# Strassen groups of the SwiGLU downs: weight sums as additions, two of four made by adding DMAs

## The chip, the core and the metric

The kernel runs on one NeuronCore of a Trainium2 chip. TensorE multiplies matrices, VectorE and ScalarE work element by element, GpSimd is used for small things, SyncE issues transfers, and 16 DMA engines move data between DRAM and the on-chip memory. The metric is the device time of one execution in microseconds (us), less is better.

## The reference

One decoder layer for 256 tokens of width 1024, in float32: a SwiGLU feed-forward, a mixer of two parallel branches (a state-space branch and differential attention), and a second feed-forward, each between two RMS norms. The part that matters here is the feed-forward, which occurs twice:

```python
def swiglu(x, w_gate, w_up, w_down):          # x: 256 x 1024, d_ff = 2816
    return (jax.nn.silu(x @ w_gate) * (x @ w_up)) @ w_down

h = h + 0.5 * rmsnorm(swiglu(rmsnorm(h, ffn1_pre_g[l]), ffn1_w_gate[l], ffn1_w_up[l], ffn1_w_down[l]), ffn1_post_g[l])
```

The product with `w_down` (2816 x 1024) is called the downs.

## The kernel before

**Precision.** Each float32 operand is split into a high part (a rounding copy on ScalarE, `whi` or `wqh`) and a low part (the difference, on VectorE, `wlo` or `wql`). A product is three TensorE products: high by high, high by low, low by high.

**Weights.** All weights arrive as chunks of 1 MB, in a list made ahead of time (`chunks`). SyncE issues their loads in that order (`load_to`, L238) into three buffers, `raw`. A chunk's buffer is given to the chunk three places on as soon as the chunk is split, so a load waits on the split that empties its buffer, and everything behind it on SyncE's queue waits too. The split parts go into a pool of 29 buffers of 4 KB per partition (`k4`), which TensorE empties by using them. Splits run ahead of their use by three chunks (`AHEAD`).

**The downs.** The rows of `w_down` make eleven chunks of 256 rows. Six of them form three Strassen groups of two chunks (class `Quad`); the order of work is the string `DOWN`: group, plain chunk, group, plain chunk, group, three plain chunks. A group is a 2 x 2 block product: two halves of its 512 rows by two halves of the 1024 columns. Quarters 0 and 1 are the left and right half of its first chunk, 2 and 3 those of its second. Seven products of 128 x 512 outputs replace eight, so a group takes 42 matmuls where its two chunks alone would take 48; a product needs either a quarter or a sum of quarters as weights. Products 1, 2 and 3 take quarters 0, 2 and 3. Products 5, 6, 7 and 4 take sums, which VectorE makes by subtraction (L122): 5 is quarter 1 less quarter 0, 6 is quarter 3 less sum 5, 7 is quarter 3 less quarter 1, and 4 is quarter 2 less sum 6. Each is one instruction on 128 x 1024 elements into a k4 buffer named `wt`. The products run in the order `FIRST` in the first two groups of a feed-forward and `LAST` in the third:

```python
FIRST, LAST = (1, 2, 3, 5, 7, 6, 4), (1, 6, 7, 2, 5, 3, 4)
```

The activations have sums of their own (`sums_of`, L674 to L677), and at the end `combine` adds product banks (L721).

**What sets the order.** Where the kernel calls `own_order`, the named engines run in the order in which the program records its instructions; elsewhere a planner of the framework orders them by costs of its own. Each engine takes its instructions strictly in order. The splits of the first group stand between the last gate and up products, whose banks (`pj`, three of them) ScalarE and VectorE empty (L330, L331).

**The end of the downs.** The last three plain chunks are held (`TAIL`), and their products run first for the upper 128 tokens, then for the lower, so that the upper block's norm runs beside the lower block's products. The gain row for the norm is loaded by GpSimd's queue (L587).

Of the kernel before, what the change touches and what calls it, by code (L numbers as in the profile page):

```python
# [19 lines left out]
ALU = mybir.AluOpType  # L20
# [6 lines left out]
P = 128  # L27
T = 256
# [26 lines left out]
def tile_hybrid_layer(ctx: ExitStack, tc: tile.TileContext, x, ffn1_pre_g, ffn1_w_gate, ffn1_w_up,  # L55
# [4 lines left out]
    nc = tc.nc  # L60
# [5 lines left out]
    def k4(shape, name, dt=F32):  # L66
        return sb.tile(shape, dt, tag="k4", name=name, bufs=K4_BUFS)
# [25 lines left out]
    class Quad:  # L93

        PLAIN = {1: 0, 2: 2, 3: 3}
        SUMS = {5: (1, 0), 6: (3, 5), 7: (3, 1), 4: (2, 6)}

        def __init__(self, i, products):  # L100
            self.i, self.sums, self.products = i, {}, products
            self.uses = [[p for p in products if p in (1, 5)], [p for p in products if p in (5, 7)],
                         [p for p in products if p in (2, 4)], [p for p in products if p in (3, 6, 7)]]

        def quarter(self, n, p):

            self.uses[n].remove(p)
            return raws[self.i + n // 2][:, :, (n % 2) * 512:(n % 2 + 1) * 512]

        def give_back(self):  # L110
            for j in range(2):
                if raws[self.i + j] is not None and not self.uses[2 * j] and not self.uses[2 * j + 1]:
                    raws[self.i + j] = None
                    load_to(self.i + j + 1 + RAW_BUFS)

        def sum_of(self, p):

            if p not in self.sums:
                n, m = self.SUMS[p]
                m = self.sum_of(m) if p in (6, 4) else self.quarter(m, p)  # L120
                t = k4([P, 2, 512], f"wt{self.i}{p}")
                nc.vector.tensor_sub(t, self.quarter(n, p), m)  # L122
                self.sums[p] = t
            return self.sums[p]

        def split(self, p):
            load_to(self.i + 2)
            hi = k4([P, 2, 512], f"wqh{self.i}{p}", F32R)
            src = self.quarter(self.PLAIN[p], p) if p in self.PLAIN else self.sum_of(p)
            nc.scalar.copy(hi, src)  # L130
            for later in self.products[self.products.index(p) + 1:][:1]:
                if later in self.SUMS:
                    self.sum_of(later)
            lo = k4([P, 2, 512], f"wql{self.i}{p}", F32R)
            nc.vector.tensor_sub(lo, src, hi.bitcast(F32))  # L135
            self.give_back()
            return lambda kt: hi[:, kt, :], lambda kt: lo[:, kt, :]

    chunks, units = [], []

    def chunk(src, shape):
        units.append((len(chunks), None))
# [8 lines left out]
    def n_chunk(w, k0):  # L153
        chunk(w[k0:k0 + 2 * P, :].rearrange("(j p) c -> p j c", p=P), [P, 2, D])

    def quad(w, k0, products):

        n = len(units)
        for k in (k0, k0 + 2 * P):
            n_chunk(w, k)  # L160
        del units[n:]
        q = Quad(len(chunks) - 2, products)
        units.extend((q, p) for p in products)


# [53 lines left out]
    raws, splits = [], []  # L219
# [11 lines left out]
    def load_to(n):  # L231
        while len(raws) < min(n, len(chunks)):
            i = len(raws)
            src, shape = chunks[i]
            r = sb.tile(shape, F32, tag="raw", name=f"raw{i}", bufs=RAW_BUFS)
            nj = shape[1] // 4 if i == 0 else shape[1] // 2 if i < 4 else shape[1]
            for j in range(0, shape[1], nj):
                nc.sync.dma_start(r[:, j:j + nj, :], src[:, j:j + nj, :])  # L238
            raws.append(r)

    def split_steps(ahead=True):


        i, _ = units[len(splits)]
        load_to(i + 1)
        r, shape = raws[i], chunks[i][1]
        nj = shape[1] // 2
        his, los = [], []
        splits.append((his, los))
        for q in range(2):  # L250
            hi = k4([P, nj, shape[2]], f"whi{i}{q}", F32R)
            lo = k4([P, nj, shape[2]], f"wlo{i}{q}", F32R)
            his.append(hi)
            los.append(lo)
            n = 1 if i == 0 else nj
            for j in range(0, nj, n):
                js = slice(j, j + n)
                copy = nc.scalar.copy if i + q + j else nc.vector.tensor_copy
                behind(copy(hi[:, js, :], r[:, q * nj + j:q * nj + j + n, :]), "cast")  # L259
                if not i + q + j:  # L260
                    yield
                m = nc.vector.tensor_sub(lo[:, js, :], r[:, q * nj + j:q * nj + j + n, :], hi[:, js, :].bitcast(F32))  # L262
# [404 lines left out]
    def sums_of(g, even, odd):  # L667


        bs = (slice(0, P), slice(P, T))  # L670
        v = k4([P, 4, 2, P], f"sv{g}")
        hi, lo = ((k3 if g < 3 else k4)([P, 3, 2, P], f"s{n}{g}", F32R) for n in "hl")
        more = k2([P, 2, 2, P], f"s4{g}", F32R)
        nc.vector.tensor_tensor(v[:, 0], even[:, :, bs[1]], odd[:, :, bs[1]], ALU.add)  # L674
        nc.vector.tensor_sub(v[:, 2], even[:, :, bs[0]], even[:, :, bs[1]])
        nc.vector.tensor_sub(v[:, 1], v[:, 0], even[:, :, bs[0]])
        nc.vector.tensor_sub(v[:, 3], odd[:, :, bs[0]], v[:, 1])  # L677
        split(hi, lo, v[:, 0:3])
        split(more[:, 0], more[:, 1], v[:, 3])
        return ([hi[:, i] for i in range(3)] + [more[:, 0]], [lo[:, i] for i in range(3)] + [more[:, 1]])  # L680

    def mm_quads(acts, sums, tag):


        bank = {p: bg([P, 512], f"acc_{tag}p{p}") for p in (2, 3, 5, 4, 8)}
        bank.update({p: pj(f"acc_{tag}p{p}") for p in (1, 6, 7)})
        acc = [[bank[2], bank[3]], [bank[4], bank[8]]]
        begun, n_quads = set(), max(n for n, (kind, j) in enumerate(down[tag]) if kind == "q") + 1
        of_quads = down[tag][:n_quads]

        def mm(p, x_, w_, last):
            nc.tensor.matmul(bank[p], x_, w_, start=p not in begun, stop=last and p in (1, 5, 6, 7))  # L692
            begun.add(p)

        for n, (kind, j) in enumerate(of_quads):
            last = n == n_quads - 1
            if kind == "p":
                wh, wl = take()
                for kt in range(2):
                    ah, al = acts[2 * j + kt]  # L700
                    for b in range(2):
                        ts = slice(b * P, (b + 1) * P)
                        for x_, w_ in ((ah, wh), (al, wh), (ah, wl)):
                            for q in range(2):
                                p = ((2, 3), (4, 8))[b][q]
                                mm(p, x_[:, ts], w_(kt)[:, halves[q]], False)
                continue
            sh, sl = sums[j]
            for p in LAST if last else FIRST:
                wh, wl = take()  # L710
                for kt in range(2):
                    if p in (1, 2, 4):
                        k, b = {1: (0, 0), 2: (2, 0), 4: (2, 1)}[p]
                        ah, al = (x_[:, b * P:(b + 1) * P] for x_ in acts[4 * j + k + kt])
                    else:
                        ah, al = (x_[{5: 0, 6: 1, 7: 2, 3: 3}[p]][:, kt, :] for x_ in (sh, sl))
# [287 lines left out]
    for o, n, off in ((0, P, 0), (P, T, P)):  # L1004
        v = dneg[:, o:o + n]
# [371 lines left out]
    class Background:  # L1377
# [5 lines left out]
        def add(self, g):  # L1383
            self.q.append(g)
# [183 lines left out]
```

## Time and profile before

| what | value |
|---|---|
| median of three runs | 734.62 us (733.73 to 734.84) |
| profiled execution, span from first to last instruction | 732.0 us |
| TensorE busy | 724.0 us (99%) |
| VectorE busy | 609.2 us (83%) |
| ScalarE busy | 475.3 us (65%) |
| moved by DMA | 137.92 MB, mean 188 GB/s |

The profile gives the execution's span; what lies around it is the 2.6 us by which the median is longer. A row of a timeline has the start and the duration in us, the engine, the line of the kernel, the operation, and output <- inputs with shapes; a bracket at its end tells how long the engine had been idle and what ended that. PE is TensorE, DVE VectorE, ACT ScalarE, POOL GpSimd, SP SyncE. The first feed-forward's downs run from 130 to 190 us, those of the second from 666 to 725 us; their first chunks are loaded from 110 and from 646 us on.

### The profile page before, as it was taken

How to read it: one execution, taken by the hardware profiler on the slowest of the kernel's cores; microseconds unless marked ns; L12 is line 12 of the kernel's file. 1: busy time of each engine (PE TensorE's matmuls, PEld its weight loads, DVE VectorE, ACT ScalarE, POOL GpSimd, SP SyncE). 2: the span in 40 equal slices, each digit the busy share in tenths (PEclk: the TensorE clock that was granted, in tenths of full speed). 3: DMA queues.
4: the chain of work that ended last, by engine and by line, in shares of the span. 5: the costliest groups of instructions: out<-in, count | busy, mean ns of one | idle time of the engine just before them, and what ended most of it. 6: DMA issues, size and time to landing. Idle time of an engine off the chain costs nothing.

```text
span 732.0 us, 10570 instructions
## 1 busy us (share of the span) xinstructions
PE 724.0 (99%) x4025; PEld 618.4 (84%) x4025; DVE 609.2 (83%) x948; ACT 475.3 (65%) x815; POOL 37.0 (5%) x66
## 2 busy tenths in 40 slices
PE   9999999999999999999999999999999999999996
PEld 7888888888878889999888888888888888888885
DVE  6978787999979999877996997784784878779995
ACT  6656566656867676869965577772663657566562
POOL 2800000000200000000000000000010000000000
PEclk9999999999999999999999999999999999999999
DMA  8874645467673647666564664475471664654541
GB/s 290 241 247 157 225 146 203 173 210 279 182 228 118 201 146 250 187 192 207 159 221 146 215 209 147 140 246 187 129 238 35 231 195 153 227 205 145 185 185 57
DMA packets 94210, 137.92 MB, mean 188 GB/s; under 512 B 2684, under 2 KB 68304, under 8 KB 94160
## 3 DMA queue, kind: packets, MB, share of 16 engines
q1 hardware_dynamic: 91488, 129.51, 53.1%
q0 software_dynamic: 2368, 7.22, 3.2%
q8 instruction: 31, 0.51, 0.3%
q10 hardware_dynamic: 304, 0.53, 0.2%
q14 instruction: 19, 0.16, 0.1%
HBM read 136.17 MB, written 1.08 MB: 188 GB/s over the span
## 4 chain that ended last, share of the span: by engine, by line
PE 99%; DVE 0%; ACT 0%; DVEq 0%; issue 0%; ACTq 0%
PE pup_f L326 9%; PE pg_f L326 9%; PE pws L345 6%; PE pgt L345 6%; PE acc_f1p L692 5%; PE acc_f2p L692 5%; PE pxs L326 4%; PE pg_f L325 4%; PE pup_f L325 4%; PE pn_f L355 3%; PE acc_mx L614 3%; PE pn_mx L345 3%; PE pn_f L345 3%; PE pwd L345 3%; PE acc_f1p L614 2%; PE acc_f2p L614 2%
## 5 line engine op out<-in xcount | busy, mean ns | idle before, releaser
L262 DVE TENSOR_TENSOR wlo<-raw,whi 128x1024 fp32r<-128x1024 f32 (+1 forms) x222 | 262.2, 1209 | 19.5 <-ACT whi L259 18.3
L259 ACT CAST whi<-raw 128x1024 fp32r<-128x1024 f32 (+1 forms) x221 | 222.8, 1043 | 12.8 <-PE psc L1255 2.5
L326 PE MATMUL pup_f<-u_f,whi 128*128 128x512 f32 x288 | 101.5, 396 | 0.0
L326 PE MATMUL pg_f<-u_f,whi 128*128 128x512 f32 x288 | 101.3, 396 | 0.0
L325 PE MATMUL pg_f<-u_f,wlo 128*128 128x256 f32 x252 | 70.6, 280 | 0.0
L325 PE MATMUL pup_f<-u_f,wlo 128*128 128x256 f32 x252 | 70.3, 279 | 0.0
L326 PEld LDWEIGHTS pup_f<-u_f,whi 128*128 128x128 f32 x288 | 52.9, 188 | 9.9
L326 PEld LDWEIGHTS pg_f<-u_f,whi 128*128 128x128 f32 x288 | 52.8, 188 | 9.7
L325 PEld LDWEIGHTS pg_f<-u_f,wlo 128*128 128x128 f32 x252 | 47.5, 189 | 1.7
L325 PEld LDWEIGHTS pup_f<-u_f,wlo 128*128 128x128 f32 x252 | 47.5, 189 | 1.6
L326 PE MATMUL pxs<-u_mx,whi 128*128 128x512 f32 x128 | 44.6, 397 | 0.0
L130 ACT CAST wqh<-wt 128x1024 fp32r<-128x1024 f32 x24 | 25.3, 1054 | 23.3 <-DVE wt L122 22.1
L330 ACT COPY su_f<-pup_f 128x256 f32<-128x256 f32 x36 | 13.4, 372 | 37.5 <-PE pup_f L326 37.4
L331 DVE TENSOR_TENSOR su_f<-pup_f,su_f 128x256 f32<-128x256 f32 x36 | 15.1, 421 | 25.0 <-ACT su_f L330 24.9
L345 PE MATMUL pgt<-whi,u_mx 128*128 128x512 f32 x128 | 33.1, 393 | 0.0
L311 PE MATMUL pz<-u_mx,whi 128*128 128x256 f32 x128 | 31.8, 285 | 0.0
L312 PE MATMUL pz<-u_mx,whi 128*128 128x256 f32 x128 | 31.4, 283 | 0.0
L325 PE MATMUL pxs<-u_mx,wlo 128*128 128x256 f32 x112 | 31.2, 279 | 0.0
L135 DVE TENSOR_TENSOR wql<-wt,wqh 128x1024 fp32r<-128x1024 f32 x24 | 29.2, 1218 | 0.2
L345 PEld LDWEIGHTS pgt<-whi,u_mx 128*128 128x128 f32 x128 | 23.6, 188 | 5.3 <-issue 0.7
L326 PEld LDWEIGHTS pxs<-u_mx,whi 128*128 128x128 f32 x128 | 23.2, 188 | 4.2
L301 ACT CAST gh_f<-sg_f 128x512 fp32r<-128x512 f32 x18 | 11.2, 620 | 23.0 <-DVE sg_f L848 23.0
(415 smaller groups left out, 1699.1 us busy)
## 6 DMA issues: line engine op xcount, KB each, us to landing
raw<-in_w_in_dram SPq DMA_DIRECT2D x40, 1024.0 KB, 5.2
raw<-in_ffn_w_down_dram SPq DMA_DIRECT2D x22, 1024.0 KB, 4.9
raw<-in_ffn_w_gate_dram SPq DMA_DIRECT2D x20, 1024.0 KB, 5.2
raw<-in_ffn_w_up_dram SPq DMA_DIRECT2D x20, 1024.0 KB, 5.2
raw<-in_ssd_w_branch_dram SPq DMA_DIRECT2D x8, 1024.0 KB, 4.9
acb<-acd POOLq DMA_DIRECT2D x8, 512.0 KB, 5.0
raw<-in_da_w_branch_dram SPq DMA_DIRECT2D x4, 1024.0 KB, 4.9
raw<-in_w_out_dram SPq DMA_DIRECT2D x4, 1024.0 KB, 4.9
```

Of the source, the lines that this page charges most:

```text
L130: nc.scalar.copy(hi, src)
L135: nc.vector.tensor_sub(lo, src, hi.bitcast(F32))
L259: behind(copy(hi[:, js, :], r[:, q * nj + j:q * nj + j + n, :]), "cast")
L262: m = nc.vector.tensor_sub(lo[:, js, :], r[:, q * nj + j:q * nj + j + n, :], hi[:, js, :].bitcast(F32))
L311: nc.tensor.matmul(acc[m], wh(j)[:, cs], ah(k0 + j), start=first and j == ks[0], stop=False)
L312: nc.tensor.matmul(acc[m], wh(j)[:, cs], al(k0 + j), start=False, stop=False)
L325: nc.tensor.matmul(acc[:, :T], wl(j)[:, cs], ah(j), start=False, stop=False)
L326: nc.tensor.matmul(acc, wh(j)[:, cs], ahl(j), start=j == 0, stop=j == KD - 1)
L345: nc.tensor.matmul(acc, a(k0 + j), b(j), start=first and i == 0, stop=last and i == 11)
L355: nc.tensor.matmul(accs[b], x_(k0 + j), w_(j), start=first and j == 0 and w_ is wh and x_ is acts[b][0], stop=last and j == 3 and w_ is wl)
L614: nc.tensor.matmul(acc[b][q][:, cs] if to is None else to, x_[:, ts], w_(kt)[:, halves[q]][:, cs], start=to is not None and kt == 0 and x_ ...
L692: nc.tensor.matmul(bank[p], x_, w_, start=p not in begun, stop=last and p in (1, 5, 6, 7))
```

## The change

The signs of the group's intermediate products are turned so that every sum of weights is an addition. Product 5 now takes quarter 0 + quarter 1, product 7 takes quarter 1 + quarter 3, product 6 takes quarter 0 + sum 7, product 4 quarter 2 + sum 6. The first two are made while loading: right after the group's first chunk has been issued, GpSimd issues a DMA that adds quarter 0 from DRAM onto quarter 1 in the chunk's buffer; SyncE loads quarter 1 once more into a k4 buffer, and GpSimd issues a DMA that adds quarter 3 from DRAM onto it. Quarter 1 is thus only used by product 5, and quarter 3 only by product 3 and, from DRAM, by sum 7. A sum's k4 buffer is taken when the chunk is loaded, not when VectorE would have made the sum. Sums 6 and 4 stay on VectorE. In the activations' sums and in `combine`, additions and subtractions change places.

```diff
-        PLAIN = {1: 0, 2: 2, 3: 3}
-        SUMS = {5: (1, 0), 6: (3, 5), 7: (3, 1), 4: (2, 6)}
+        PLAIN = {1: 0, 5: 1, 2: 2, 3: 3}
...
-            self.uses = [[p for p in products if p in (1, 5)], [p for p in products if p in (5, 7)],
-                         [p for p in products if p in (2, 4)], [p for p in products if p in (3, 6, 7)]]
+            self.uses = [[p for p in products if p in (1, 6)], [5], [p for p in products if p in (2, 4)], [3]]
...
+        def of_dram(self, k, c):
+            return self.w[self.k0 + k * T:self.k0 + (k + 1) * T, c * 512:(c + 1) * 512].rearrange(
+                "(j p) c -> p j c", p=P)
+
+        def added(self):
+
+            nc.gpsimd.dma_start(raws[self.i][:, :, 512:], self.of_dram(0, 0), accum_op=ALU.add)
+            t = self.sums[7] = k4([P, 2, 512], f"wt{self.i}7")
+            nc.sync.dma_start(t, self.of_dram(0, 1))
+            nc.gpsimd.dma_start(t, self.of_dram(1, 1), accum_op=ALU.add)
...
-                n, m = self.SUMS[p]
-                m = self.sum_of(m) if p in (6, 4) else self.quarter(m, p)
+                n, m = {6: (0, 7), 4: (2, 6)}[p]
+                m = self.sum_of(m)
                 t = k4([P, 2, 512], f"wt{self.i}{p}")
-                nc.vector.tensor_sub(t, self.quarter(n, p), m)
+                nc.vector.tensor_tensor(t, self.quarter(n, p), m, ALU.add)
...
             raws.append(r)
+            if i in quads:
+                quads[i].added()
...
-        nc.vector.tensor_tensor(v[:, 0], even[:, :, bs[1]], odd[:, :, bs[1]], ALU.add)
+        nc.vector.tensor_sub(v[:, 0], even[:, :, bs[1]], odd[:, :, bs[1]])
...
-        nc.vector.tensor_sub(v[:, 3], odd[:, :, bs[0]], v[:, 1])
+        nc.vector.tensor_tensor(v[:, 3], odd[:, :, bs[0]], v[:, 1], ALU.add)
...
-            add(u4, bank[5], u2)
-            add(c4, bank[5], u3)
+            nc.vector.tensor_sub(u4, bank[5], u2)
+            nc.vector.tensor_sub(c4, bank[5], u3)
```

In each engine's list of instructions, VectorE has 850 rows before and 838 after, GpSimd 70 and 82, SyncE 127 and 133; TensorE has the same 3220, of which in each feed-forward two (the first two matmuls of the first group's product 2) move from between the last two up-products' halves to behind them.

More of the change, by code (lines that the diff above doesn't have):

```diff
@@ L93, in tile_hybrid_layer, with __init__ @@
     class Quad:
-        PLAIN = {1: 0, 2: 2, 3: 3}
-        SUMS = {5: (1, 0), 6: (3, 5), 7: (3, 1), 4: (2, 6)}
-        def __init__(self, i, products):
-            self.i, self.sums, self.products = i, {}, products
-            self.uses = [[p for p in products if p in (1, 5)], [p for p in products if p in (5, 7)],
-                         [p for p in products if p in (2, 4)], [p for p in products if p in (3, 6, 7)]]
+        PLAIN = {1: 0, 5: 1, 2: 2, 3: 3}
+        def __init__(self, i, w, k0, products):
+            self.i, self.w, self.k0, self.sums, self.products = i, w, k0, {}, products
+            self.uses = [[p for p in products if p in (1, 6)], [5], [p for p in products if p in (2, 4)], [3]]
         def quarter(self, n, p):
@@ L131, in split @@
             for later in self.products[self.products.index(p) + 1:][:1]:
-                if later in self.SUMS:
+                if later in (4, 6):
                     self.sum_of(later)
@@ L137, in split @@
             return lambda kt: hi[:, kt, :], lambda kt: lo[:, kt, :]
-    chunks, units = [], []
+    chunks, units, quads = [], [], {}
     def chunk(src, shape):
@@ L161, in quad @@
         del units[n:]
-        q = Quad(len(chunks) - 2, products)
+        q = quads[len(chunks) - 2] = Quad(len(chunks) - 2, w, k0, products)
         units.extend((q, p) for p in products)
```

## The prediction

> **What bounds the kernel now.** I read the page first (busy shares, then the chain that ended last), then TensorE's waits, then the stretch of the first feed-forward's downs in windows.
>
> ```profile
> span 732.0 us, 10570 instructions
> PE 724.0 (99%) x4025; PEld 618.4 (84%) x4025; DVE 609.2 (83%) x948; ACT 475.3 (65%) x815; POOL 37.0 (5%) x66
> ...
> PE 99%; DVE 0%; ACT 0%; DVEq 0%; issue 0%; ACTq 0%
> ```
> ```profile
> PE warm L425 <- DVE zeros L408: 1.1, 1, 1.1
> PE pn_f L355 <- DVE raw_u L478: 0.3, 1, 0.3
> ```
> ```profile
> core 0: us, PE busy (x) PEld busy (x) DVE busy (x) ACT busy (x) POOL busy (x), PEclk, DMA share, GB/s
> 110.00:120.00 10.00, 10.00 (x59) 8.73 (x58) 7.79 (x10) 7.28 (x11) 0.00 (x0) 1.00 0.65 221
> 120.00:130.00 10.00, 10.00 (x60) 8.69 (x58) 8.13 (x11) 5.64 (x8) 0.00 (x0) 1.00 0.38 147
> 130.00:140.00 10.00, 10.00 (x50) 8.40 (x49) 9.93 (x12) 6.61 (x9) 0.00 (x0) 1.00 0.56 210
> 140.00:150.00 10.00, 10.00 (x46) 8.29 (x45) 9.04 (x9) 5.79 (x7) 0.00 (x0) 1.00 0.42 131
> 150.00:160.00 10.00, 10.00 (x45) 8.28 (x45) 9.87 (x9) 5.58 (x6) 0.00 (x0) 1.00 0.71 249
> 160.00:170.00 10.00, 10.00 (x45) 8.26 (x44) 9.96 (x10) 7.53 (x9) 0.53 (x1) 1.00 0.44 148
> ```
> TensorE is the chain. In the whole run it waited 1.4 us, all near the start, and in the downs it is busy 10.00 of every 10 us at full clock, although VectorE is nearly as full (9.0 to 10 from 130 us on). VectorE is behind, but never late for TensorE. The span is 732.0 us; the runs' median 734.62 lies 2.6 above it, so I add whatever I find to 734.6.
>
> **The change, part by part.**
>
> *VectorE sums removed.* A feed-forward has three groups of four sums; two of each four go.
>
> ```profile
> L122 DVE TENSOR_TENSOR wt<-raw,wt x12: 1210/1215/1225, 130.5 to 702.2; 128x1024 f32<-128x1024 f32 x12
> L122 DVE TENSOR_TENSOR wt<-raw x6: 1212/1216/1220, 124.1 to 692.8; 128x1024 f32<-128x1024 f32 x6
> L122 DVE TENSOR_TENSOR wt<-raw,raw x6: 1216/1217/1220, 127.0 to 696.4; 128x1024 f32<-128x1024 f32 x6
> ```
> ```profile
> ACT wqh L130 <- DVE wt L122: 22.1, 18, 3.2
> ```
> The last two rows go: 12 x 1.216 = 14.6 us of VectorE. ScalarE's 22.1 us of waiting for sums shrinks with them. Neither is on the path: TensorE did not wait for them, so the gain is 0, and the matmuls are as many as before (in each feed-forward only two move, from inside the last up-product to behind it). Turning an add into a subtract in the activation sums and at the end leaves engine, count and shape alone: 0.
>
> *Transfers added.* Per group: one plain load of 512 KB on SP's queue, and two adding loads of 512 KB on GpSimd's. Per feed-forward 3 plain, 6 adding. In the six windows the DMA share sums to 3.16, so 31.6 us of DMA time moved (221+147+210+131+249+148) x 10 us = 11.06 MB: 2.86 us per MB. A 1 MB chunk takes 3.0 us of DMA time, a plain 512 KB 1.5.
>
> An adding load is nowhere in the trace. Call its DMA time a. Lower end: 1.5, a plain load of the same bytes (it cannot move less, so no gain below that). Upper end: 4.5, if source read, destination read and write follow one another without overlap. I take 3.0: for one write the DMA engine reads twice, and the plain 1.5 already holds one read with its write overlapped.
>
> A page of the Trainium skill speaks against the change here: Collectives: The Full Stack, section "The bandwidth ceiling: the fold count and why AG ≠ RS ≠ AR", says that the add in the datapath costs no cycles but needs two source reads, and gives 62.28 against 32.35 GB/s, 1.93 times. By that, as an estimate, a is 2.9 and the sum below would be 741.4; no run here shows it yet.
>
> *GpSimd's queue.*
>
> ```profile
> L1159 POOL DMA_DIRECT2D acb<-acd x8: 527/530/569, 279.9 to 348.5; - x8
> ...
> DMA to landing us min/median/max: 4.0/5.0/6.0
> ```
> ```profile
> 168.65 0.53 POOL L587 DMA_DIRECT2D pg_f<-in_ffn_post_g_dram  x1 [135.22 <-PE acc_f1p L692]
> ```
> ```profile
> L555 DVE TENSOR_TENSOR og_f<-p_f,pg_f x2: 683/687/691, 180.9 to 716.2; 128x512 f32<-128x512 f32 x2
> ```
> Six issues at 0.53 are 3.2 us in a queue that idles 135 us: free. Behind them stands only the gain row's load, issued at 168.65 and used at 180.9; it has 6 us over a 6.0 landing.
>
> *SP's queue.* Its order around the downs (start, duration of issue):
>
> ```profile
> 109.64 0.37 SPq L238 DMA_DIRECT2D raw<-in_ffn_w_down_dram  x1
> ...
> 116.74 2.97 SPq L238 DMA_DIRECT2D raw<-in_ffn_w_down_dram  x2
> ...
> 128.28 0.37 SPq L238 DMA_DIRECT2D raw<-in_ffn_w_down_dram  x1
> ...
> 147.49 0.37 SPq L238 DMA_DIRECT2D raw<-in_ffn_w_down_dram  x1
> ...
> 161.42 0.37 SPq L238 DMA_DIRECT2D raw<-in_ffn_w_down_dram  x1
> ...
> 168.32 0.37 SPq L238 DMA_DIRECT2D raw<-in_ffn_w_down_dram  x1
> ```
> ```profile
> 142.35 0.39 PE L692 MATMUL acc_f1p<-wql,gh_f 128*128 128x512 f32 x1
> ```
> The third group's plain load needs a k4 buffer that TensorE frees with the first group's last matmul (142.35); behind it on SP waits a chunk that was issued at 147.49 anyway. 5 us of cover, so 0.
>
> *First place where it can bite: the first group's second chunk.* A chunk lands 4.9 us after its issue, so the first (109.64) about 114.5; its adding load then enters the DMA queue ahead of, or beside, the second chunk (116.74).
>
> ```profile
> raw<-in_ffn_w_down_dram SPq DMA_DIRECT2D x22, 1024.0 KB, 4.9
> ```
> ```profile
> 121.58 1.05 ACT L130 CAST wqh<-raw 128x1024 fp32r<-128x1024 f32 x1 [1.96 <-DMA raw<-in_ffn_w_down_dram]
> ```
> ```profile
> 143.93 1.22 DVE L122 TENSOR_TENSOR wt<-raw 128x1024 f32<-128x1024 f32 x1
> 145.07 1.22 DVE L135 TENSOR_TENSOR wql<-raw,wqh 128x1024 fp32r<-128x1024 f32 x1
> ```
> ```profile
> 113.08 0.69 DVE L302 TENSOR_TENSOR gl_f<-sg_f,gh_f 128x512 fp32r<-128x512 f32 x1 [0.69 <-ACT gh_f L301]
> ```
> ```profile
> L331 DVE TENSOR_TENSOR su_f<-pup_f,su_f 128x256 f32<-128x256 f32 x36 | 15.1, 421 | 25.0 <-ACT su_f L330 24.9
> ```
> ```profile
> 130.23 0.40 PE L692 MATMUL acc_f1p<-wqh,gh_f 128*128 128x512 f32 x1
> ```
> ScalarE took that chunk the moment it landed, 121.58; with one adding load ahead that is 121.6 + a. In the new order the gate bank is then emptied after one cast (1.05), three low parts (pitch 145.07 - 143.93 = 1.14 each), a 0.69 low part of the activations and its own 0.42 add: 5.6 us. The last up-product, which needs that bank, now starts at 130.23 (the place of the moved matmuls). Slack 130.23 - 5.6 - 121.6 = 3.0. At a = 3.0 the stall is 0; at 4.5 it is 1.5; with two adding loads ahead it would be 3.0 even at 3.0.
>
> *Second place: the last chunk of the downs.*
>
> ```profile
> 173.22 2.01 ACT L259 CAST whi<-raw 128x1024 fp32r<-128x1024 f32 x2 [1.17 <-DMA raw<-in_ffn_w_down_dram]
> ```
> ```profile
> 174.31 2.36 DVE L262 TENSOR_TENSOR wlo<-raw,whi 128x1024 fp32r<-128x1024 f32 x2 [0.27 <-ACT whi L259]
> ```
> ```profile
> 175.67 0.42 PE L614 MATMUL acc_f1p<-wlo,gh_f 128*128 128x512 f32 x1
> ```
> ```profile
> 709.50 2.00 ACT L259 CAST whi<-raw 128x1024 fp32r<-128x1024 f32 x2 [1.17 <-DMA raw<-in_ffn_w_down_dram]
> ```
> The chunk issued at 168.32 lands as ScalarE begins on it (173.22), its low part ends at 174.31 + 1.2 = 175.5, and TensorE uses it at 175.67. The slack is 0.1 us; every us that this chunk lands after 173.2 is a us of the kernel. The second feed-forward has the same at 709.50.
>
> When does it land afterwards? DMA work from the first adding load (about 116.7) to its end: ten chunks x 3.0 = 30.0, two plain loads 3.0, six adding loads 6a, the gain row 1.5 (it gets in front once the chunk is later than 168.65): 34.5 + 6a. Idle stretches which the order forces: 4.0 before the fourth chunk (as now: the two chunks issued from 116.74 on are home by about 119.4 + 4.9 = 124.3, the next goes out at 128.28), since its buffer waits for the first group's sums; and 2.8 before the tenth, whose buffer is now held until the third group's fifth split: six VectorE steps x 1.14 = 6.9 after an adding load is home, plus 1.9 for landing and starting (4.9 less the 3.0 of moving), less the a + 3.0 = 6.0 that the queue still has. Landing takes some 0.7 of that 1.9 at the end. Sum: 116.7 + 34.5 + 6a + 6.8 + 0.7 = 158.7 + 6a, against 173.2. No stall below a = 2.4; 3.5 us at 3.0; 12.5 at 4.5.
>
> *Behind it.* In the first feed-forward two splits of the next stage's weights move ahead of the first norm's add on VectorE: 2 x 1.14 = 2.3 at most, 0 if those weights are early. With late chunks they are not: I take 1.0.
>
> Sum: 2 x (0 + 3.5) + 1.0 = 8.0; 734.6 + 8.0 = 742.6.
>
> **The rivals.** *Hidden after all (not slower).* If the DMA engines take an adding load nearly as a plain one (a up to 2.4), the last chunk lands by 173.2 and TensorE never waits: 734.6. For it: DMA is busy only 31.6 of 60 us, and at 1.5 the additions make it 45; VectorE, freed, hands buffers back earlier. Against: 0.1 us of slack at the last chunk.
> *DMA becomes the bound.* At a = 4.5, 31.6 + 4.5 + 27 = 63 us of DMA work stand in a 60 us stretch: 1.5 + 12.5 twice, and 2 behind: 764.6. For it: landings on GpSimd's queue are already 4.0 to 6.0 for 1.5 of moving. Against: nothing shows that reads and write do not overlap.
> *Faster.* TensorE's rate would have to rise; its 1.4 us of waits are not here. At best some tenths: 734.
>
> **How the numbers follow.** A measurement here tells 0.2% (1.5 us) from no change. Forecast (a from 2.4 to 4): 0.44. Hidden: 0.26. DMA-bound (a of 4 and more, or two adding loads ahead): 0.26. Faster by over 0.2%: 0.04. So slower 0.70, same 0.26. The range goes from 734.0 to 765 (a = 4.5), leaving out some 0.08 below and 0.12 above; the likeliest case alone spans 736 to 757.
>
> **What would show it.** VectorE's sum group at 12 instead of 24; adding loads on GpSimd's queue with a landing of 4 to 6 plus a - 1.5; DMA share of 110 to 170 near 0.9; TensorE waiting for wlo and whi in the last three chunks of each downs, little elsewhere. Wrong if: adding loads land within 6 us and the DMA share stays near 0.75 (then 734.6), or if TensorE stalls at the last up-product by several us (then over 755).

## The result, and the profile after

The changed kernel takes 752.50 us (median of four runs, 750.59 to 754.28) where the kernel before takes 734.17: a ratio of 1.0248, 95% interval 1.0233 to 1.0262. The forecast was 742.6 with a range of 734 to 765. Slower was right and the range holds the time; the loss is 18.3 us where 8.0 were worked out.

The head of the page after and its chain that ended last:

```profile
span 750.5 us, 10607 instructions
...
PE 731.1 (97%) x4025; PEld 619.8 (83%) x4025; DVE 597.5 (80%) x936; ACT 474.7 (63%) x815; POOL 51.7 (7%) x78
...
PE 82%; DMA 10%; DVE 4%; issue 2%; ACT 1%; SPq 0%; DVEq 0%; POOLq 0%; ACTq 0%
```

The span has grown by 18.5 us. TensorE was the whole chain before; now DMA holds 10% of it. VectorE is 11.7 us less busy. TensorE's waits after the change (what waits, for what, us in total, how often, the longest):

```profile
PE pup_f L337 <- DVE sg_f L342: 3.5, 2, 2.1
PE acc_f2p L625 <- ACT whi L270: 2.3, 1, 2.3
PE acc_f2p L703 <- DVE wql L144: 2.1, 2, 1.7
PE acc_f1p L703 <- DVE wql L144: 1.7, 3, 0.6
PE warm L436 <- DVE zeros L419: 1.1, 1, 1.1
PE acc_f1p L625 <- DVE wlo L273: 1.1, 3, 0.5
PE pu_mx L481 <- DVE h L594: 0.9, 1, 0.9
PE acc_f2p L625 <- DVE wlo L273: 0.4, 1, 0.4
```

They stand in four places: the last up-product (`pup_f`), the third group (`wql`), the last plain chunks (`whi`, `wlo`) and the norm (`pu_mx`). Of these rows only the warm-up's was there before. What decides the total, however, is one place, the last chunk of each downs. ScalarE's casts after the change:

```profile
182.13 2.00 ACT L270 CAST whi<-raw 128x1024 fp32r<-128x1024 f32 x2 [0.49 <-DMA raw<-in_ffn_w_down_dram]
```
```profile
728.38 2.00 ACT L270 CAST whi<-raw 128x1024 fp32r<-128x1024 f32 x2 [0.48 <-DMA raw<-in_ffn_w_down_dram]
```

Before, these casts began at 173.22 and 709.50. The first is 8.9 us late; the second 18.9, of which 10.0 (8.9 and the norm's 1.1) are carried over from the first downs. 8.9 + 1.1 + 8.9 = 18.9 us is the loss, within 0.4 us of what the span has grown by. In this kernel a stall further up does not come on top: after the first of them TensorE is 3.9 us behind (a matmul of the first group that started at 135.78 starts at 139.71), after the last chunk 8.9 us, and the last chunk would have held it up that long anyway. This is read from the times of the one trace; it was not tried by itself.

Why is the last chunk late? The stretch from the first adding load to its landing, whole and then cut at its idle places (windows of the changed kernel: TensorE busy, weight loads, VectorE, ScalarE, GpSimd, granted clock, DMA share, GB/s):

```profile
116.70:182.10 65.40, 61.09 (x278) 49.23 (x277) 47.70 (x49) 36.07 (x45) 7.46 (x7) 0.97 0.80 235
```
```profile
116.70:118.30 1.60, 1.60 (x11) 1.42 (x11) 1.60 (x2) 1.60 (x4) 1.60 (x2) 1.00 0.00 0
118.30:130.20 11.90, 11.90 (x70) 10.29 (x68) 6.54 (x9) 5.26 (x8) 0.55 (x1) 1.00 1.00 264
130.20:134.70 4.50, 2.44 (x12) 1.91 (x11) 4.50 (x7) 2.42 (x6) 0.00 (x0) 0.87 0.02 3
134.70:153.30 18.60, 18.60 (x80) 15.43 (x80) 12.71 (x14) 10.29 (x13) 2.37 (x2) 0.94 0.95 273
153.30:156.40 3.10, 3.10 (x15) 2.58 (x14) 2.61 (x3) 2.11 (x2) 0.68 (x1) 1.00 0.32 70
156.40:171.30 14.90, 14.33 (x64) 11.53 (x63) 11.10 (x10) 6.96 (x7) 1.69 (x2) 1.00 0.96 280
171.30:176.50 5.20, 4.38 (x18) 2.73 (x16) 3.50 (x4) 2.78 (x3) 0.57 (x1) 1.00 0.43 137
176.50:182.10 5.60, 4.75 (x19) 3.32 (x19) 5.14 (x6) 4.65 (x6) 0.00 (x0) 1.00 0.97 359
```

The DMA engines were busy for 0.80 x 65.4 = 52.3 us. The prediction had 34.5 + 6a = 52.5 at a = 3.0. They were idle for 13.1 us, where it had 6.8 (and 0.7 for landing). The rows say where: 1.6 while the first adding load is issued and set up, 4.4 before the fourth chunk (4.50 x 0.98), 2.1 before the seventh, 3.0 before the tenth. The second and the fourth of these were in the sum with 4.0 and 2.8; the first and the third were not; the remaining 2 us are small gaps in the full rows.

### The profile page after: what moved, and what is told of

Same layout as the page of the kernel before. It is cut to its first block, busy times and chain, and to the rows that moved or that the text cites. A ratio compares the mean times of both kernels' runs of the same rounds, so it can differ in the third digit from the quotient of the medians.

```text
span 750.5 us, 10607 instructions
## 1 busy us (share of the span) xinstructions
PE 731.1 (97%) x4025; PEld 619.8 (83%) x4025; DVE 597.5 (80%) x936; ACT 474.7 (63%) x815; POOL 51.7 (7%) x78
## 3 DMA queue, kind: packets, MB, share of 16 engines
q0 software_dynamic: 5632, 13.52, 8.0%
## 4 chain that ended last, share of the span: by engine, by line
PE 82%; DMA 10%; DVE 4%; issue 2%; ACT 1%; SPq 0%; DVEq 0%; POOLq 0%; ACTq 0%
PE pup_f L337 8%; PE pg_f L337 7%; PE pws L356 6%; PE pgt L356 6%; DMA raw<-in_ffn_w_down_dram 6%; PE pxs L337 4%; DMA wt<-in_ffn_w_down_dram 4%; PE pup_f L336 3%; PE pg_f L336 3%; PE pn_mx L356 3%; PE acc_mx L625 3%; PE pn_f L366 3%; PE pn_f L356 3%; PE pwd L356 3%; PE pz L322 2%; PE pz L325 2%
## 5 line engine op out<-in xcount | busy, mean ns | idle before, releaser
L337 PE MATMUL pup_f<-u_f,whi 128*128 128x512 f32 x288 | 103.2, 401 | 3.5 <-DVE sg_f L342 3.5
L144 DVE TENSOR_TENSOR wql<-raw,wqh 128x1024 fp32r<-128x1024 f32 x24 | 28.6, 1220 | 10.8 <-ACT wqh L139 10.3
L139 ACT CAST wqh<-wt 128x1024 fp32r<-128x1024 f32 x18 | 18.7, 1050 | 28.2 <-DVE wt L131 18.0
L139 ACT CAST wqh<-raw 128x1024 fp32r<-128x1024 f32 x24 | 24.3, 1049 | 12.8 <-DMA raw<-in_ffn_w_down_dram 12.2
L131 DVE TENSOR_TENSOR wt<-raw,wt 128x1024 f32<-128x1024 f32 x12 | 14.6, 1220 | 15.2 <-DMA wt<-in_ffn_w_down_dram 10.6
```

The source lines that it names most:

```text
L337: nc.tensor.matmul(acc, wh(j)[:, cs], ahl(j), start=j == 0, stop=j == KD - 1)
```

## The experiments

Each diff is against the changed kernel unless it says otherwise. The kernel before was run beside each group of runs (733.6 to 734.4 us); ratios are to that.

### The second read: plain loads, and twice as many

**Plain.**

```diff
-            nc.gpsimd.dma_start(raws[self.i][:, :, 512:], self.of_dram(0, 0), accum_op=ALU.add)
+            nc.gpsimd.dma_start(raws[self.i][:, :, 512:], self.of_dram(0, 0))
...
-            nc.gpsimd.dma_start(t, self.of_dram(1, 1), accum_op=ALU.add)
+            nc.gpsimd.dma_start(t, self.of_dram(1, 1))
```

> The changed kernel with the add left out of its twelve GpSimd loads: the same loads by the same queues into the same places, plain, so that products 5 and 7 take wrong weights (the output is not the reference's). Theory A (the second read of an adding load, 3.0 us of DMA time instead of 1.5): DMA busy time of 110 to 170 us falls from 49.8 to about 41 us, the second chunk of the first group lands about 3 us earlier, and the time is 735 to 738 us. Rival B (the added bytes, the queue on GpSimd and the longer holding of buffers, not the adding): 748 us or more.

734.22 us, ratio 1.0011 (0.9999 to 1.0023). The added bytes, queues and waits of the change and the sums that VectorE no longer makes come to nothing together; all 18.3 us come with the add. Theory A stands here, with a time a little under its 735, and rival B falls. The last chunk is cast from 173.09 us on, as early as in the kernel before. The window up to there, with plain loads:

```profile
116.70:173.20 56.50, 56.50 (x271) 47.30 (x270) 48.30 (x49) 35.68 (x45) 4.30 (x7) 1.00 0.76 272
```

The DMA engines were busy for 0.76 x 56.5 = 42.9 us and idle for 13.6, no less than in the changed kernel (13.1). So the add did not make the idle time. It put 52.3 - 42.9 = 9.4 us more DMA work into a stretch whose idle time did not shrink to take it up, and the last chunk came 9.0 us later (182.13 against 173.09).

GpSimd's queue, from the DMA section of three pages (packets, MB, the time that the packets took as a share of 16 engines' span): the kernel before, the plain loads, the changed kernel:

```profile
q0 software_dynamic: 2368, 7.22, 3.2%
```
```profile
q0 software_dynamic: 4096, 13.52, 6.0%
```
```profile
q0 software_dynamic: 5632, 13.52, 8.0%
```

Over their spans these are 23.4, 43.9 and 60.0 us. A plain load of 512 KB so takes (43.9 - 23.4) / 12 = 1.7 us of DMA time, an adding one (60.0 - 23.4) / 12 = 3.05, for the same bytes in (5632 - 2368) / (4096 - 2368) = 1.9 times the packets. The Trainium skill (Collectives: The Full Stack, "The bandwidth ceiling: the fold count and why AG ≠ RS ≠ AR") has the add in the datapath need two source reads, 1.93 times a plain transfer; here it is 3.05 / 1.7 = 1.8 times by time and 1.9 times by packets. The trace agrees that an adding load is nearly two plain ones; the factor by time is a little below the page's, and the measurement decides.

The whole adding load also lands later. The DMA section's landing rows on GpSimd's queue, changed kernel first, then with plain loads (issuing line's queue, count, KB, median us from issue to landing):

```profile
raw<-in_ffn_w_down_dram POOLq DMA_DIRECT2D x6, 512.0 KB, 8.5
wt<-in_ffn_w_down_dram POOLq DMA_DIRECT2D x6, 512.0 KB, 11.4
```
```profile
raw<-in_ffn_w_down_dram POOLq DMA_DIRECT2D x6, 512.0 KB, 6.1
wt<-in_ffn_w_down_dram POOLq DMA_DIRECT2D x6, 512.0 KB, 7.4
```

**Two plain transfers for each adding one.** Is it the DMA time, or something slow in the add itself?

```diff
-            nc.gpsimd.dma_start(raws[self.i][:, :, 512:], self.of_dram(0, 0), accum_op=ALU.add)
+            self.twice(raws[self.i][:, :, 512:], self.of_dram(0, 0), 5)
...
-            nc.gpsimd.dma_start(t, self.of_dram(1, 1), accum_op=ALU.add)
+            self.twice(t, self.of_dram(1, 1), 7)
+
+        def twice(self, to, src, p):
+            nc.gpsimd.dma_start(dram.tile([P, 2, 512], F32, tag=f"x{self.i}{p}", name=f"x{self.i}{p}"),
+                                raws[self.i][:, :, :512])
+            nc.gpsimd.dma_start(to, src)
```

> The changed kernel with each adding load replaced by two plain transfers of 512 KB on GpSimd's queue: first quarter 0 of the chunk's buffer out to an unused place in DRAM, then the plain load (no add: products 5 and 7 take wrong weights). The DMA engines so have the 3.0 us of work of an adding load as two plain transfers. Theory A (an adding load costs by its DMA time, twice a plain one, and nothing else): 748 to 754 us, with the DMA share of 110 to 170 us near 0.83 and a stall at the last up-product. Rival G (an adding load has a latency or a serial path of its own that plain transfers do not have): 735 to 742 us at the same DMA share.

752.02 us, ratio 1.0234 (1.0185 to 1.0282): the changed kernel's time. Its window over the same stretch:

```profile
116.70:182.10 65.40, 60.02 (x275) 48.77 (x273) 46.32 (x47) 34.41 (x44) 8.65 (x13) 0.97 0.80 279
```

The DMA share is 0.80 as in the changed kernel. An adding load costs the kernel as much as two plain transfers, and nothing peculiar to the add is needed (rival G falls). The single runs lie between 747.2 and 755.1 us, so the two kernels are the same only to within some us. The run does not part the DMA time from the time to landing either: its last transfers into `raw` and `wt` land 8.9 and 11.6 us after their issue in the median, the adding ones 8.5 and 11.4.

### Which group pays: one group adding, the others plain

```diff
+            kw = dict(accum_op=ALU.add) if self.k0 == 1 * 2 * T else {}
-            nc.gpsimd.dma_start(raws[self.i][:, :, 512:], self.of_dram(0, 0), accum_op=ALU.add)
+            nc.gpsimd.dma_start(raws[self.i][:, :, 512:], self.of_dram(0, 0), **kw)
...
-            nc.gpsimd.dma_start(t, self.of_dram(1, 1), accum_op=ALU.add)
+            nc.gpsimd.dma_start(t, self.of_dram(1, 1), **kw)
```

(2 and 3 in place of 1 for the second and the third group.)

> The kernel with plain loads (734.22 us), in which the first group of each feed-forward alone adds as it loads (products of groups 2 and 3 so take wrong weights). Theory H (one chain of transfers runs from the first group to the last chunk; second reads are paid by what is not taken up in idle stretches that the order forces): the two stretches between this group and the last chunk take up most of the 3 us: 734.5 to 738 us, with a stall at the last up-product of 2 us that the later groups make up or not. Rival A (each group pays in its own place, and the stall at the last up-product is lasting): 738 to 740 us.

> The same with the second group alone adding. Theory H: 735 to 740 us, more than for the first group. Rival A (no place of its own in the second group showed a wait in the changed kernel): 734 to 735 us.

> The same with the third group alone adding. Theory H: the largest of the three, since the last chunk's load waits for product 5 of this group, whose weights an adding load makes: 740 to 745 us, and the three single groups together (each less 734.2) come to less than the changed kernel's 18.3 us by what idle stretches take up. Rival A: third group's waits 2.7 and 2.6 and the last chunks' 2.2 and 4.7: 746 us.

| adding group | us | ratio (95%) | over 734.22 |
|---|---|---|---|
| first | 736.72 | 1.0039 (1.0025 to 1.0053) | 2.5 |
| second | 742.36 | 1.0118 (1.0099 to 1.0136) | 8.1 |
| third | 742.62 | 1.0105 (1.0074 to 1.0136) | 8.4 |

Theory H holds in that the first group costs little; the second and the third are not told apart. The second group pays 8.1 us although the changed kernel shows hardly a wait in its products: it delays the last chunk, which is cast from 178.66 instead of 173.09. Rival A's three numbers are all missed. Two parts of H are misses too: the second group lies above its 735 to 740, and the three should have come to less than 18.3 and come to 19.0, which the spread of the runs (740.9 to 744.3 and 739.4 to 744.7) does not tell from 18.3.

TensorE's wait at the last up-product, with the first group adding and with the second group adding:

```profile
PE pup_f L338 <- DVE sg_f L343: 1.8, 1, 1.8
```
```profile
PE pup_f L338 <- DVE sg_f L343: 1.9, 1, 1.9
```

Both stand in the first feed-forward. In the first of these runs the last chunk is on time there (cast from 172.98), and the stall lasts: the matmul that started at 135.78 in the kernel before starts at 139.44, and the whole span is 2.9 us longer (734.9 against 732.0). So the first group's 2.5 us are this one stall with the half clock behind it, and on this point rival A was right. The second run has the stall although its first group loads plainly: ScalarE took the first group's second chunk at 127.04, where it was 124.54 with plain loads throughout. The stall so comes without the add as well, for a reason that these traces do not show, and part of the second group's 8.1 us may be it.

### The idle stretches: four chunk buffers

```diff
-K4_BUFS = 29
+K4_BUFS = 27
...
-RAW_BUFS = 3
+RAW_BUFS = 4
```

> The changed kernel with four chunk buffers instead of three, and 27 instead of 29 of the smaller buffers to make room. Theory H (the DMA engines' idle stretches before the fourth, seventh and tenth chunk come from the three buffers, and turn a DMA work that would just fit into 9 us of lateness per feed-forward): the idle time from the first adding load to the last chunk falls from 13 to under 8 us, 737 to 744 us. Rival A (the second reads cost by their DMA time or latency whatever the buffers): 749 to 754 us.

> The control: the kernel before with four chunk buffers and 27 smaller ones. Theory H and rival A: the same as the kernel before within 0.5%, 733 to 737 us, since TensorE has nothing to win; if it comes out slower by more, two smaller buffers fewer cost something, which then stands in e15 too.

With the adding loads: 732.71 us, ratio 0.9990 (0.9981 to 1.0000). The kernel before with the same buffers: 736.02, ratio 1.0031 (1.0018 to 1.0044). The loss of 18.3 us is gone, more than theory H forecast. The window from the first adding load to the time at which the last chunk used to land, first in this kernel, then in the kernel before, and TensorE's waits in this kernel:

```profile
116.70:173.20 56.50, 56.50 (x272) 47.47 (x271) 50.70 (x52) 39.46 (x48) 5.31 (x5) 1.00 0.89 273
```
```profile
116.70:173.20 56.50, 56.50 (x273) 47.45 (x272) 53.42 (x55) 36.10 (x44) 0.53 (x1) 1.00 0.54 191
```
```profile
PE warm L436 <- DVE zeros L419: 1.1, 1, 1.1
PE pn_f L366 <- DVE raw_u L489: 0.3, 1, 0.3
```

Nearly the same DMA work, 0.89 x 56.5 = 50.3 us of it, now fits into the 56.5 us that TensorE needs, with 6.2 us idle instead of 13.1, and TensorE waits no more than in the kernel before. So the second read is not too much work. With three buffers a load goes out only after its buffer's chunk is split, and in this stretch the DMA engines stood idle for some 13 us with plain and with adding loads alike; with four buffers this halves. The control shows that the two smaller buffers fewer do not help: they go with a time that is longer by 0.3%. The 0.1% by which the adding version is ahead of the kernel before is within what is called no change here; against the control with the same buffers it is 3.3 us ahead.

### What the sums on VectorE are worth: the signs without the transfers

```diff
-        PLAIN = {1: 0, 5: 1, 2: 2, 3: 3}
+        PLAIN = {1: 0, 2: 2, 3: 3}
+        SUMS = {5: (0, 1), 7: (1, 3), 6: (0, 7), 4: (2, 6)}
...
-                n, m = {6: (0, 7), 4: (2, 6)}[p]
-                m = self.sum_of(m)
+                n, m = self.SUMS[p]
+                m = self.sum_of(m) if p in (6, 4) else self.quarter(m, p)
```

(`added` does nothing, and `uses` lists the products that take each quarter.)

> The changed kernel with its turned signs, but sums 5 and 7 made on VectorE again (additions of raw quarters), no transfer added. Theory A (the adding transfers are the whole cost): 734 us, within 0.2% of the kernel before, TensorE waits about 1.4 us. Rival C (the turned signs and the order of the sums, quarter 0 needed until product 6, have a price of their own): 736 us or more, with TensorE waiting in the groups.

742.55 us, ratio 1.0123 (1.0106 to 1.0139). Theory A missed. Rival C was right in the time: the turned signs by themselves cost 8.7 us in this order of products, with no transfer added. It was wrong in the place: TensorE waits for `whi` in the last plain chunks (1.7 and 1.6 us), not in the groups. Two other orders of products were tried for it. The first, on top of this edit:

```diff
-FIRST, LAST = (1, 2, 3, 5, 7, 6, 4), (1, 6, 7, 2, 5, 3, 4)
+FIRST, LAST = (1, 2, 3, 5, 7, 6, 4), (1, 6, 7, 5, 2, 3, 4)
```

> The kernel with turned signs and all sums on VectorE (742.55 us), with the third group's products in the order 1, 6, 7, 5, 2, 3, 4 instead of 1, 6, 7, 2, 5, 3, 4. Theory E (that kernel's 8.7 us come from the third group's first chunk, which the turned signs need until product 5, so that its buffer's next load goes out some 3 us late and the last chunk with it): 734 to 737 us, the load that was issued at 164.6 goes out near 161.5 to 162.5. Rival C (another price of the turned sums, such as sum 7 being needed ahead of sum 6): 741 to 743 us.

741.89 us, ratio 1.0103 (1.0088 to 1.0118). A miss for theory E: the load meant still went out at 164.56. The second, on top of the first:

```diff
+SECOND = (1, 5, 7, 6, 2, 3, 4)
...
-            for p in LAST if last else FIRST:
+            for p in LAST if last else SECOND if j == QUADS[tag][1] else FIRST:
```

> Turned signs, all sums on VectorE, third group in the order 1, 6, 7, 5, 2, 3, 4 (that alone gave 741.89 us), and now the second group in the order 1, 5, 7, 6, 2, 3, 4 instead of 1, 2, 3, 5, 7, 6, 4. Theory E2 (the longer hold costs in the second group: its first chunk is needed until sum 6 is made, so the third group's first chunk, issued at 147.49 before, goes out at 150.05): that load goes out by 147.5, the last chunk is issued by 168.5, 734 to 736 us. Rival C (the turned sums cost by VectorE's work or order elsewhere): 739 to 742 us.

741.30 us, ratio 1.0110 (1.0079 to 1.0140). A miss again: the third group's first chunk did go out earlier, at 147.18, but the last chunk only at 170.29. What is left is VectorE itself. With the old signs sum 5 needs the first chunk of a group alone, and sum 6 takes it; with the new ones sum 6 takes sum 7, and sum 7 needs the second chunk. The third group runs product 6 second, so its first sum waits for the second chunk. Moving product 5 ahead fills that time (on top of the run before):

```diff
-FIRST, LAST = (1, 2, 3, 5, 7, 6, 4), (1, 6, 7, 5, 2, 3, 4)
+FIRST, LAST = (1, 2, 3, 5, 7, 6, 4), (1, 5, 7, 6, 2, 3, 4)
```

> Turned signs, all sums on VectorE, the order 1, 5, 7, 6, 2, 3, 4 in the second group and now in the third too (1, 6, 7, 5, 2, 3, 4 gave 741.30 us). Theory F (in the third group sums 7 and 6 both need the second chunk, where the old signs let one of them be made ahead of it; VectorE, which has no slack from there to the last chunk, stood idle 1.4 us at 156.4 for it): sum 5, which needs the first chunk alone, fills that idle time, the last chunk's cast starts by 174.5 instead of 176.5, 734 to 737 us. Rival C2 (some other price of the signs): 740 to 742 us.

733.60 us, ratio 1.0000 (0.9990 to 1.0010). Theory F holds, with a time a little under its 734. VectorE around the third group's first sum in the run before this one, then with product 5 second:

```profile
154.12 2.35 DVE L283 TENSOR_TENSOR wlo<-raw,whi 128x1024 fp32r<-128x1024 f32 x2
157.84 1.23 DVE L140 TENSOR_TENSOR wt<-raw,raw 128x1024 f32<-128x1024 f32 x1 [1.37 <-PE acc_f1p L713]
```
```profile
154.23 2.35 DVE L283 TENSOR_TENSOR wlo<-raw,whi 128x1024 fp32r<-128x1024 f32 x2
156.50 1.22 DVE L140 TENSOR_TENSOR wt<-raw 128x1024 f32<-128x1024 f32 x1
157.64 1.22 DVE L154 TENSOR_TENSOR wql<-raw,wqh 128x1024 fp32r<-128x1024 f32 x1
158.78 1.22 DVE L140 TENSOR_TENSOR wt<-raw,raw 128x1024 f32<-128x1024 f32 x1
```

And ScalarE's cast of the last chunk in the same two kernels:

```profile
176.49 1.99 ACT L280 CAST whi<-raw 128x1024 fp32r<-128x1024 f32 x2 [2.48 <-DMA raw<-in_ffn_w_down_dram]
```
```profile
172.91 2.00 ACT L280 CAST whi<-raw 128x1024 fp32r<-128x1024 f32 x2 [1.09 <-DMA raw<-in_ffn_w_down_dram]
```

In the first, VectorE stands idle for 1.37 us ahead of sum 7 (157.84); in the second a sum that needs the first chunk alone (156.50) and a low part come in between, and it never stops. The last chunk is 3.6 us earlier. That the order repairs the loss is shown; that the idle time is its cause is only argued. The bracket of the row names a matmul and not the second chunk, and which of the two ended the idle time the trace does not settle. In the run with the old order (742.55 us) VectorE is idle for only 0.37 us ahead of sum 7 and 0.87 us later on; there the last chunk goes out 1.8 us late (170.11 against 168.32) and lands 6.8 us after its issue instead of 4.8. In the kernel with plain loads the same signs in the old order cost nothing: there 12 sums are off VectorE. In that order, then, loading sums 5 and 7 instead of making them on VectorE is worth 742.55 - 734.22 = 8.3 us, and the turned signs give just that away.

### Some groups on VectorE, some by adding loads

These two ran before the above was known; both count groups on VectorE as free, which with these signs and this order they are not. The edit holds the one with all sums on VectorE; its further lines:

```diff
+            self.dma = (5, 7) if k0 == 2 * T else ()
...
-            nc.gpsimd.dma_start(raws[self.i][:, :, 512:], self.of_dram(0, 0), accum_op=ALU.add)
+            if 5 in self.dma:
+                nc.gpsimd.dma_start(raws[self.i][:, :, 512:], self.of_dram(0, 0), accum_op=ALU.add)
+            if 7 not in self.dma:
+                return
```

> Adding loads in the first group of each feed-forward alone; groups 2 and 3 make sums 5 and 7 on VectorE. Theory A (three separate places pay): the stall at the last up-product stays, 2.3 and 1.8 us, with the 1.5 us of half clock behind the first; the third group and the last chunks pay nothing: 734.2 + 5.5 = 739 to 740 us. Rival D (the loss is one backlog of the DMA queues that grows over the groups, and begins at the first group): the time is the same 739 to 740 or less, but the third group still waits by some tenths.

743.80 us, ratio 1.0129 (1.0108 to 1.0150), which is not told from the kernel with all sums on VectorE (742.55). A miss for both theories: the price of the signs is in the total, and the stall of the first group, which was there (1.6 us in the first feed-forward), hardly adds to it.

The other way round, `() if k0 == 2 * T else (5, 7)`:

> Adding loads in groups 2 and 3 of each feed-forward; the first group makes sums 5 and 7 on VectorE. Theory A (three separate places pay): no stall at the last up-product; the third group still costs 2.7 and 2.6 us, the last chunks 2.2 and 4.7 with half clock, the norm 1.1: 734.2 + 13.3 = 747.5 us. Rival D (one backlog that begins at the first group): without the first group's loads the later groups are on time, 734 to 739 us.

750.32 us, ratio 1.0225 (1.0205 to 1.0246): only 2.2 us less than with all three groups adding. Rival D's backlog from the first group falls; theory A is nearer, with its number 2.8 us too low.

Sum 7 alone by an adding load, sum 5 on VectorE (`self.dma = (7,)`):

> The changed kernel with sum 7 by an adding load and sum 5 on VectorE: three adding loads per feed-forward instead of six, none into a chunk's own buffer. Theory A (adding loads cost by DMA time, one ahead of the second chunk fits the slack): no stall at the last up-product, no wait in the third group, and the last chunk pays by the longer hold of the third group's first chunk and by the six sums that VectorE keeps: 738 to 743 us. Rival D (any adding load on the path costs the same): half of the changed kernel's 18.3 on top of the signs' price, 747 us or more.

739.42 us, ratio 1.0067 (1.0052 to 1.0082), as theory A had it; rival D falls. With three adding loads in a downs, of which the first goes out beside the first group's second chunk (117.64 and 117.74), there is no wait at the last up-product and none in the third group; the last plain chunks have waits of 1.9 us.

### One adding load ahead of the second chunk

```diff
+
+        def added_7(self, second):
+
             t = self.sums[7] = k4([P, 2, 512], f"wt{self.i}7")
-            nc.sync.dma_start(t, self.of_dram(0, 1))
+            m = nc.sync.dma_start(t, self.of_dram(0, 1))
+            tc.add_manual_dep(m.ins, second.ins.name, order, reason="behind the second chunk")
...
+            if i - 1 in quads:
+                quads[i - 1].added_7(m)
```

> The changed kernel with one edit: SyncE issues the plain load of quarter 1 for sum 7 behind the group's second chunk, not ahead of it, so the second adding load, which waits for it, starts only after that chunk; one adding load instead of two stands ahead of the second chunk. Theory A (my slack of 3.0 us at the first place was right, and two adding loads ahead of the chunk overran it): the second chunk lands at 124.5 to 125.5 instead of 126.9, TensorE waits at most 0.5 us at the last up-product, no half clock there, 747 to 749 us. Rival D (a backlog that is only shifted): the first group pays in its products 7 and 6 what it saves, and the time stays at 751 to 754 us.

766.29 us, ratio 1.0452 (1.0435 to 1.0470). The place that the edit aimed at behaved as theory A said: the second chunk was taken at 122.87 instead of 126.94, and TensorE did not wait at the last up-product. But the third group, whose second product takes sum 6 and so needs sum 7, now waits for it, once in each feed-forward:

```profile
PE acc_f1p L709 <- ACT wqh L143: 9.8, 1, 9.8
PE acc_f2p L709 <- ACT wqh L143: 8.8, 1, 8.8
```

Both totals were missed. This run decides nothing between A and D, since the edit made a wait of its own.

## Why the prediction was right or wrong

**TensorE bounds, removed sums are worth 0.** The net of the VectorE part came out at 0 by luck. The prediction took "VectorE is behind, but never late for TensorE" as slack, and it took the turned signs at 0. Signs turned with all sums on VectorE, in the old order, cost 8.7 us; taking two sums of four off VectorE (the plain loads) brings the time back to 734.22. The prediction's own windows have VectorE at 9.87 and 9.96 of 10 us from 150 to 170: that is no slack. What the prediction put at 0 twice was a tie between two terms of 8 us.

**The DMA time of an adding load.** Right: 3.05 us against the 3.0 taken. The landing was not: 8.5 and 11.4 us, where the prediction's sign, 4 to 6 plus a - 1.5, makes 5.5 to 7.5.

**GpSimd's queue.** An adding load's issue is not the 0.53 us of the row that was used:

```profile
L117 POOL DMA_DIRECT2D wt<-in_ffn_w_down_dram x6: 1179/1190/1508, 117.3 to 699.9; - x6
```

It is 1.18 to 1.51. That it is hidden was right: GpSimd is busy for 7% of the span, and no instruction waits for the gain row, which is issued at 172.33. **SyncE's queue.** Right: the third group's plain load went out at 146.70, ahead of a chunk that waited until 155.09 for its buffer anyway.

**First place.** The chain was right: ScalarE takes the second chunk at 126.94 and the last up-product starts at 132.52, 5.6 us later as worked out.

```profile
126.94 2.00 ACT L139 CAST wqh<-raw 128x1024 fp32r<-128x1024 f32 x2 [4.49 <-DMA raw<-in_ffn_w_down_dram]
```
```profile
132.52 0.50 PE L337 MATMUL pup_f<-u_f,whi 128*128 128x512 f32 x1 [2.06 <-DVE sg_f L342]
```

The stall of 0 was wrong: two adding loads (116.34 and 117.34) went out ahead of this chunk (117.50), the case for which the prediction named 3.0 us, and TensorE waited 2.06. In the changed kernel this stall is overtaken by the lateness at the end, so it is not added to the total; in the run with the first group alone, where the last chunk is on time, it lasts.

**Second place: this is the step that failed by size.** The rule was right (a us of the kernel for each us that the last chunk lands late, 0.1 us of slack) and so was the DMA work, 52.3 us against 52.5. The term that was mis-sized is the idle time, 6.8 us and 0.7 for landing where the trace has 13.1. Its 4.0 before the fourth chunk and 2.8 before the tenth were 4.4 and 3.0. Missing altogether were 1.6 us before the first adding load moves anything and 2.1 us before the seventh chunk, which waits for the second group's product 6 and so for an adding load of its own, and some 2 us of small gaps. So 8.9 us per downs instead of 3.5. The add is not what the sum had wrong. With plain loads, at a = 1.7, it gives 158.7 + 6 x 1.7 = 168.9, and the last chunk is cast at 173.1, 4.2 us later; at 3.05 it gives 177.0, and the cast is at 182.1, 5.1 us later. The idle time that the sum lacks is there in both. The sum treated the queue as one line of work with two holes in it; it is a loop, in which a late load delays a split, the split a buffer, and the buffer the next load. The run with four buffers loosens that loop, and the loss is gone.

**Norm.** 1.0 was taken, 1.1 measured, but late chunks are not the reason: with plain loads, where the last chunk is on time, TensorE waits there for 0.8 us too.

**The rivals.** Hidden after all needed a up to 2.4: the plain loads, at 1.7, come out at its 734, and the changed kernel does not meet the condition. DMA as the bound: two adding loads ahead of the chunk, one of its conditions, did occur, but a was 3.05 and not 4 or more, and four buffers make the same work fit.

## What to carry to other kernels

In a pipeline with few buffers idle DMA time is not room for more transfers: here 13.6 us were idle and 9.4 us more work did not fit. Walk the loop load, split, buffer, next load once around for every chunk and look for each load that waits on something which the change makes later. One more buffer can be worth more than the traffic saved; try it before giving up the change. And when instructions are taken off an engine that is "never late", undo the removal alone while keeping the rest of the change: two terms may cancel, and the order of the products is then free to be set anew.

## What the runs showed of the hardware

TensorE's granted clock fell to half after stalls of some 2 us. Windows of the changed kernel, each 3.4 us long, a stall and what follows it, once in each feed-forward:

```profile
130.10:133.50 3.40, 1.34 (x9) 0.94 (x8) 3.40 (x5) 1.79 (x4) 0.00 (x0) 1.00 0.01 4
133.50:136.90 3.40, 3.40 (x12) 2.92 (x12) 2.15 (x5) 2.91 (x5) 0.00 (x0) 0.50 0.65 180
724.00:727.40 3.40, 1.11 (x5) 0.48 (x3) 0.57 (x2) 1.49 (x2) 0.00 (x0) 1.00 0.71 293
727.40:730.80 3.40, 3.02 (x8) 1.84 (x7) 3.29 (x4) 2.50 (x3) 0.00 (x0) 0.50 0.01 6
```

TensorE was busy for 39% and 33% of a window and had the clock at 0.50 for the whole of the next. The first time 2.06 us of waiting became 3.9 us of lateness by 139.71 us. The Trainium skill (TensorE: Matmul & The Clock Gate, "HAM oscillation — how this bites in real kernels") warns of idle gaps of more than about 3.4 us; here 2.06 us of idle time within one window were enough, and the measurement decides. Not every such stall does it: in the run with the second group adding, a wait of 1.87 us at the same place left the clock at 1.00, and these runs were not made to find what decides. How much of the 18.3 us the half clock makes was not tried; the run with adding loads in the first group alone has it behind its stall too, and costs 2.5 us in all.
